# Packed first loads, another order of the first projection, and hand-placed side products in a two-layer decoder step

## The chip, the cores and the metric

The kernel runs on one core of one Trainium2 chip. A core has five engines that run beside each other and wait for one another through semaphores: TensorE (PE in the profile; PEld are its weight loads), VectorE (DVE), ScalarE (ACT), GpSimd (POOL) and SyncE (SP), which issues most of the transfers. Sixteen DMA engines carry the transfers of all queues. The metric is the device time of one execution in microseconds (us). Before the change it is 618.79 us, the median of three runs (618.44 to 619.36).

## What is computed

One inference step of a decoder with two layers, for 256 prompt rows and 8 sample rows (one new token each, with 256 past tokens in pages of 128) that share all weights. In fp32; model width 1024, 8 heads of 64 per attention, feed-forward width 2816.

```python
# layer 0                                         # for prompt rows and sample rows
h = rmsnorm(x, norm_g);  z = h @ w_in             # w_in: 1024 x 2560
q, k, v, bu, bv = split(z)                        # 512 columns each
q, k = rope(q), rope(k)
a = softmax(q k^T / 8, causal, incl. past) v      # 256-blocks; with these sizes all past is seen
bvn = layer_norm(gelu(bv), sgu_gain)
b = gelu(bu) * (tril(sgu_w) @ bvn + sgu_b)        # mixes rows in chunks of 128
x = x + concat(a, b) @ w_out                      # 1024 x 1024
x = x + (gelu(causal_conv3(h2 @ w_gate)) * (h2 @ w_up)) @ w_down,  h2 = rmsnorm(x)
# layer 1: the same frame with w_in of 1024 x 2048 (q, k, v, u), stick-breaking attention
# and a pooling mixer; at the end a final rmsnorm
```

Outputs are the normed rows, the new k and v, the new bvn rows of the samples, and the pooling and convolution states.

## The kernel before

**Layout.** Everything is held transposed: a tile of 128 features by 264 columns (256 prompt rows and 8 sample rows). A weight is cut into blocks of 128 x 128; the host packs the 1472 blocks in the order in which they are used (`_phases`, line 95, and `_pack_weights`, line 123). The kernel walks that list once (`run`, line 310): block after block, three matmuls each, because both operands are split into a high part (rounded to fp32r) and a low part (the rest): high weight by high data (L329), high by low (L330), low by high (L331). So the first projection (in0) has 160 blocks and 480 matmuls, the first output projection (out0) 64 blocks and 192 matmuls. "Block 32" below is the 33rd block of that list.

**Weights.** Eight blocks are a weight tile. `raw` (line 275) loads 8 or 16 blocks by one transfer from SP's queue into a pool of three buffers (`rawp`), `split` (line 290) makes the high part `wh` on ScalarE (L306) and the low part `wl` on VectorE (L307), up to three tiles ahead, in four buffers. The first tile is split by VectorE in three pieces (L303, L304), and its load is cut in three as well. A fourth load of raw weights has to wait until the first buffer is free again.

**The first data.** The input and the norm's gain come in four transfers from ScalarE's queue (line 345). Each of the eight input tiles is multiplied by the gain and split (`operand_tile`, line 371: L373 on ScalarE, L374 on VectorE). The squares of the tiles (L386) are added up on GpSimd (L395, L398); a matmul with ones (L406) and Ln and Exp on ScalarE (L408, L409) give the factor R = 1/rms, which is applied to the results of the projection, not to its input. Eight matmuls on a constant (`warm`, L357) run before the data are there.

**The first projection.** Its order is q, k, bv, bu, v, four output tiles each (`in0`, line 97). For the first four output tiles the list goes over the five first input tiles in the outer loop (`q0`, `KQ = 5`), so that it can start with little data; then each output tile takes its eight blocks in one go. A result is in one of four PSUM banks of the pool `psm` (tag `mm`) until `in0_evac` (line 630) has taken it: for q and k a shuffle (L635), a multiplication (L637 or L639), a multiplication on GpSimd (L640) and an addition (L641), for the others one multiplication with R (L643). All need R.

**Side products.** The four other PSUM banks (`psa`, tag `at`) serve the small matmuls: scores of the prompt (`s_qk`, line 655), softmax (`s_soft`), transposes (`s_tr`), products with v (`s_av`), the same for the samples (`sm_score`, `sm_soft`, `sm_tr`, `sm_out`), and the gating mixer (`gm_mean`, `gm_var`, `gm_norm`, `gm_tr`, `gm_gate`). Each is hung on the list by a number (`hk.at`, lines 796 to 836): `hk.at(n, f)` means that f is written down after 8(n+1) blocks. What follows from that is decided by a scheduler that simulates a timeline when the kernel is built; it may put a product later, and it interleaves its matmuls with those of the list. Only what `tc.keep_in_program_order` marks stays where it is written. On the chip each engine then goes through its own list strictly in order.

**Queues.** SP's queue issues the weights, the constants, and the pages of the caches: 16 page numbers are read from the page table into registers (`value_load`, line 424) and 32 pages of 256 KB are loaded for layer 0 (K, then V). A transfer that waits for a buffer holds up what stands behind it on that queue.

Of the kernel before, what the change touches and what calls it, by code (L numbers as in the profile page):

```python
# [9 lines left out]
F32 = mybir.dt.float32  # L10
# [8 lines left out]
P = 128  # L19
# [19 lines left out]
PINM = 8  # L39
SQL = 2  # L40
XD = (1, 2, 4, 8)
WARM = 8
YD = ((0, 1), (1, 3), (3, 5), (5, 7), (7, 8))

SC0 = 9
SGL = 6
GG = 16
GM = 12
GV = 13.5
GN = 16.1  # L50
SQK = 5
STR = 7
SSO = 9.5
STP = 12
GT = 17
GA = 17.5
VP = 17
SAV = 18
AVS = 18.5
MSK = 4.5  # L60
KL = 0
VL = 9
SQ = 4
SMO = -0.5
# [30 lines left out]
def _phases():  # L95
    k8 = list(range(KD))
    in0 = [(n, t) for n in ("q", "k", "bv", "bu", "v") for t in range(4)]
# [25 lines left out]
def _pack_weights(w_in0, w_out0, w_in1, w_out1, gate, up, down):  # L123
# [28 lines left out]
    return np.concatenate(out)  # L152
# [18 lines left out]
def _consts():  # L171
# [19 lines left out]
    h8 = np.arange(8)  # L191
# [8 lines left out]
    add("sm", (used & (h32[:, None] // 2 == h8[None, :])).astype(f))  # L200
    add("hs", (used & ((2 * g32 + h32 % 2)[:, None] == (np.arange(512) // 64)[None, :])).astype(f))
# [7 lines left out]
    ("w", (_NB * P * P,)), ("x", (P, KD + KD * T)), ("vec", (P, _NVEC)), ("cst", _CST_ARR.shape), ("rope", (P, 2 * T)),  # L209
# [12 lines left out]
def tile_decoder_step(ctx: ExitStack, tc: tile.TileContext, a):  # L222
    nc = tc.nc
    v, s, g, pe = nc.vector, nc.scalar, nc.gpsimd, nc.tensor
# [22 lines left out]
    XG = con.tile([P, KD + KD * T], F32, name="XG")  # L247
    GAIN = XG[:, :KD]
    X = XG[:, KD:].rearrange("p (m t) -> p m t", t=T)
# [5 lines left out]
    PALL = con.tile([P, 4, NS, 16], F32, name="PALL")  # L255

# [17 lines left out]

    def raw(ci):
        if ci not in raws:
            n = _CHUNKS[ci] * P
            r = rawp.tile([P, n], F32, tag="raw", name=f"raw{ci}")
            o = coff[ci] * P * P
            src = a["w"][o:o + P * n].rearrange("(p f) -> p f", p=P)  # L280
            raws[ci] = r
            if ci == 0:
                return lambda c, e: nc.sync.dma_start(r[:, c * P:e * P], src[:, c * P:e * P])
            nc.sync.dma_start(r, src)
        return raws[ci]
# [4 lines left out]
    def split(t):  # L290
        for tt in range(len(splits), min(t + (LOOK if pos[0] else 0), NT - 1) + 1):
# [5 lines left out]
            h = wsp.tile([P, 8 * P], F32R, tag="wh", name=f"wh{tt}")  # L297
            l = wsp.tile([P, 8 * P], F32R, tag="wl", name=f"wl{tt}")
            splits[tt] = (h, l)
            if tt == 0:  # L300
                def piece(c, e, h=h, l=l, src=src):
                    c, e = c * P, e * P
                    tc.keep_in_program_order(v.tensor_copy(h[:, c:e], src[:, c:e]))  # L303
                    tc.keep_in_program_order(v.tensor_tensor(l[:, c:e], src[:, c:e], h[:, c:e].bitcast(F32), ALU.subtract))  # L304
                return piece
            s.activation(h, src, AF.Copy)  # L306
            v.tensor_tensor(l, src, h.bitcast(F32), ALU.subtract)  # L307
        return splits[t]

    def run(order, rhs, evac, hooks=None):  # L310
# [5 lines left out]
        for m, k in order:  # L316
# [4 lines left out]
            if m not in ps:  # L321
                ps[m] = psm.tile([P, 512], F32, tag="mm", name=f"mm{i}")
                first = True
            else:
                first = False
# [9 lines left out]
            while hooks and n >= 8 * (hooks[0][0] + 1):  # L335
                for f in hooks.pop(0)[1]:
                    f()

    orders = dict(_PHASES)


    CS = f4("ropecs", (P, 2, T))
    xcut = [0] + [KD + e * T for e in XD]
    for b, e in zip(xcut, xcut[1:]):
        nc.scalar.dma_start(XG[:, b:e], a["x"][:, b:e])
    part = raw(0)
    part(0, 2)
    part(2, 4)
    part(4, 8)
    raw(1)  # L350
    raw(2)
    s.preload_act_table_set("natural_log_exp_and_others")
    warm = con.tile([P, 512], BF16, name="warm")
    v.memset(warm, 1.0)
    pw = at("warm")
    for i in range(WARM):
        tc.keep_in_program_order(pe.matmul(pw, warm[:, :P], warm, start=i == 0, stop=i == WARM - 1))  # L357

    def late(dst, src):
# [729 lines left out]
```

## Time and profile before

| what | value |
|---|---|
| median of 3 runs | 618.79 us |
| the profiled execution | 618.47 us |
| its span, first to last instruction | 616.4 us |
| mean granted TensorE clock | 0.996 |
| weight transfers of 1024 KB | 89, of 512 KB 5 |
| DMA moved | 121.40 MB, mean 197 GB/s |
| start of block 0, 32, 160 and 192 (first matmul of each) | 4.51, 24.92, 90.57, 110.39 us |

The span is the stretch from the first to the last instruction; the 2.1 us by which the execution is longer lie around it. In the views each row of a group gives the line of the kernel, the engine, the operation, what is written and read, its shape and count, then busy time and mean duration. A matmul is pipelined: the duration in its row (some 280 ns) is longer than the distance from one matmul to the next (some 120 ns), so what a matmul costs is read from start to start. On VectorE and ScalarE, too, the next instruction starts before the one in front of it ends, by some 0.08 to 0.1 us. An idle time in brackets names what ended it.

### The profile page before, as it was taken

How to read it: one execution, taken by the hardware profiler on the slowest of the kernel's cores; microseconds unless marked ns; L12 is line 12 of the kernel's file. 1: busy time of each engine (PE TensorE's matmuls, PEld its weight loads, DVE VectorE, ACT ScalarE, POOL GpSimd, SP SyncE). 2: the span in 40 equal slices, each digit the busy share in tenths (PEclk: the TensorE clock that was granted, in tenths of full speed). 3: DMA queues.
4: the chain of work that ended last, by engine and by line, in shares of the span. 5: the costliest groups of instructions: out<-in, count | busy, mean ns of one | idle time of the engine just before them, and what ended most of it. 6: DMA issues, size and time to landing. Idle time of an engine off the chain costs nothing.

```text
span 616.4 us, 12351 instructions
## 1 busy us (share of the span) xinstructions
PE 599.4 (97%) x4924; PEld 575.3 (93%) x4924; DVE 413.1 (67%) x704; ACT 350.4 (57%) x621; POOL 84.9 (14%) x111
## 2 busy tenths in 40 slices
PE   7899999999999999999999999999999999999994
PEld 5788987999999999999999997899999999999994
DVE  6986663969976676655555686396996766764441
ACT  5459763767756555644442757376765555554441
POOL 3330132324200000001110000042420000001020
PEclk9999999999999999999999999999999999999998
DMA  7995873543655445695477559944364555554502
GB/s 259 325 403 220 328 258 54 206 153 133 216 184 205 158 184 205 228 392 200 155 229 262 219 184 141 134 175 172 136 215 170 200 182 167 199 189 166 200 1 70
DMA packets 41354, 121.40 MB, mean 197 GB/s; under 512 B 17490, under 2 KB 19410, under 8 KB 29906
## 3 DMA queue, kind: packets, MB, share of 16 engines
q1 hardware_dynamic: 40178, 119.00, 59.3%
q10 hardware_dynamic: 1120, 1.63, 0.9%
q8 instruction: 38, 0.62, 0.4%
q14 instruction: 18, 0.15, 0.1%
HBM read 116.67 MB, written 3.94 MB: 196 GB/s over the span
## 4 chain that ended last, share of the span: by engine, by line
PE 84%; DVE 7%; issue 3%; DMA 2%; ACT 2%; POOL 1%; SPq 0%; DVEq 0%; ACTq 0%
PE mm L330 26%; PE mm L329 25%; PE mm L331 25%; DMA raw<-in_w 2%; DVE wl L307 2%; DVE xn_l L374 1%; PE pv_l L465 1%; PE sc L451 1%; PE pav L494 1%; PE Z L900 1%; DVE wk L542 1%; ACT wh L306 1%; PE Z L884 1%; POOL wk L553 0%; PE pt L684 0%
## 5 line engine op out<-in xcount | busy, mean ns | idle before, releaser
L307 DVE TENSOR_TENSOR wl<-raw,wh 128x1024 fp32r<-128x1024 f32 x183 | 229.4, 1255 | 129.1 <-ACT wh L306 129.0
L306 ACT ACTIVATE wh<-raw 128x1024 fp32r<-128x1024 f32 x183 | 193.7, 1059 | 182.5 <-PE mm L330 169.3
L330 PE MATMUL mm<-xn_l,wh 128*128 128x264 f32 x544 | 154.7, 284 | 1.7 <-DVE xn_l L374 1.5
L329 PE MATMUL mm<-xn_h,wh 128*128 128x264 f32 x544 | 153.8, 283 | 0.0
L331 PE MATMUL mm<-xn_h,wl 128*128 128x264 f32 x544 | 153.4, 283 | 0.0
L330 PEld LDWEIGHTS mm<-xn_l,wh 128*128 128x128 f32 x544 | 102.3, 188 | 2.5 <-DVE xn_l L374 2.5
L329 PEld LDWEIGHTS mm<-xn_h,wh 128*128 128x128 f32 x544 | 102.1, 188 | 0.0
L331 PEld LDWEIGHTS mm<-xn_h,wl 128*128 128x128 f32 x544 | 102.1, 188 | 0.0
L330 PE MATMUL mm<-a_l,wh 128*128 128x264 f32 x352 | 99.8, 284 | 0.0
L329 PE MATMUL mm<-a_h,wh 128*128 128x264 f32 x352 | 99.5, 284 | 0.0
L331 PE MATMUL mm<-a_h,wl 128*128 128x264 f32 x352 | 99.4, 283 | 0.0
L331 PEld LDWEIGHTS mm<-a_h,wl 128*128 128x128 f32 x352 | 66.2, 188 | 0.0
L330 PEld LDWEIGHTS mm<-a_l,wh 128*128 128x128 f32 x352 | 66.2, 188 | 0.0
L329 PEld LDWEIGHTS mm<-a_h,wh 128*128 128x128 f32 x352 | 66.0, 188 | 0.0
L329 PE MATMUL mm<-xg_h,wh 128*128 128x264 f32 x160 | 46.6, 298 | 3.6 <-DVE q L637 1.6
L330 PE MATMUL mm<-xg_l,wh 128*128 128x264 f32 x160 | 46.1, 293 | 0.0
L331 PE MATMUL mm<-xg_h,wl 128*128 128x264 f32 x160 | 44.7, 291 | 1.3 <-DVE wl L307 1.3
L329 PE MATMUL mm<-xg_f_h,wh 128*128 128x264 f32 x160 | 45.8, 286 | 0.0
L330 PE MATMUL mm<-xg_f_l,wh 128*128 128x264 f32 x160 | 45.4, 284 | 0.0
L331 PE MATMUL mm<-xg_f_h,wl 128*128 128x264 f32 x160 | 45.3, 283 | 0.0
L329 PE MATMUL mm<-xg_n_h,wh 128*128 128x264 f32 x128 | 37.4, 292 | 0.0
L331 PE MATMUL mm<-xg_n_h,wl 128*128 128x264 f32 x128 | 36.8, 288 | 0.0
(266 smaller groups left out, 1074.5 us busy)
## 6 DMA issues: line engine op xcount, KB each, us to landing
raw<-in_w SPq DMA_DIRECT2D x89, 1024.0 KB, 4.8
K<-in_kt SPq DMA_DIRECT2D x32, 256.0 KB, 6.0
V<-in_vp SPq DMA_DIRECT2D x32, 256.0 KB, 5.6
raw<-in_w SPq DMA_DIRECT2D x5, 512.0 KB, 5.3
CST<-in_cst SPq DMA_DIRECT2D x1, 548.0 KB, 5.5
XG<-in_x ACTq DMA_DIRECT2D x1, 528.0 KB, 7.8
out_k<-k SPq DMA_DIRECT2D x1, 528.0 KB, 9.4
out_v<-v SPq DMA_DIRECT2D x1, 528.0 KB, 3.0
```

The lines of the kernel that those rows point to most:

```text
L306: s.activation(h, src, AF.Copy)
L307: v.tensor_tensor(l, src, h.bitcast(F32), ALU.subtract)
L329: pe.matmul(o, h[:, c:c + P], xh, start=first, stop=False)
L330: pe.matmul(o, h[:, c:c + P], xl, start=False, stop=False)
L331: pe.matmul(o, l[:, c:c + P], xh, start=False, stop=left[m] == 0)
L374: j = v.scalar_tensor_tensor(l, src, gain, h.bitcast(F32), ALU.mult, ALU.subtract)
L451: pe.matmul(ps[32 * t:32 * t + 32, :PAST].rearrange("p (g k) -> p g k", g=NPG), qz[:, t, sq, :], kt[sq][:, :, t * P:(t + 1) * P], start=sq ...
L465: pe.matmul(pv[32 * j:32 * j + 32, :], pz[:, pg, sq, :], vtiles[sq][:, pg, :], start=pg == 0, stop=pg == NPG - 1)
L494: pe.matmul(o, vt[:, 0, h * HD:(h + 1) * HD], w[:, :SEQ], start=True, stop=False)
L542: v.scalar_tensor_tensor(C[:, 1:SEQ], G[:, 0:SEQ - 1], wc(1, j), C[:, 1:SEQ], ALU.mult, ALU.add)
L884: tc.keep_in_program_order(pe.matmul(ps[:, 0:SEQ], kh[:, 0:P], qh[:, 0:SEQ], start=False, stop=False, skip_group_check=True))
L900: pe.matmul(ps[:, 0:384], negU, x, start=False, stop=False, skip_group_check=True)
```

## The change

The change is confined to what happens up to the end of out0, with three small exceptions named at the end.

1. **Packed first loads.** The gain, the eight input tiles and the first 16 weight blocks are packed into one array `xw` on the host (`_FIRST`, `_pack_first`) and come by six transfers, each with the weight blocks and the input tile that go together: two blocks and tile 0 with the gain, two blocks and tile 1, then three times four blocks and one tile, then tiles 5 to 7. Transfers 1 and 3 go from ScalarE's queue, the others from SP's. The weights of blocks 16 to 47 no longer go through the pool of three buffers, but into tiles of the general pool `up`. The page table comes on ScalarE's queue at the start, and the 16 page numbers are read on SP's queue between the first weight loads. The weight loads keep their written place on SP's queue. The residual needs the input once more, so it is loaded again into `X` in four transfers of 264 KB at blocks 120 to 144 (`late_x`).
2. **Order of the first projection.** bv, q, k, bu, v. ScalarE makes the high parts of the first weights but for the first two blocks; all of this is in a written order (`part`, `whole`). The norm is finished after block 30 (`norm0`); the results of the first four output tiles are held in their banks until then. The first two q tiles (blocks 32 and 40) use banks of the other pool (`spare`).
3. **Side products at chosen blocks.** `blk(b, f)` puts f after b blocks, and while `fixed` is set, which is during in0 and out0, all matmuls and transposes keep their written order. The numbers stand in the diff. The products of the probabilities with v, all four, now come after block 8 of out0.
4. **Work moved between engines.** The second multiplication of rope, the sums of squares of the gating mixer and its last multiplication go from GpSimd to VectorE; one of the two scalings of the probabilities from ScalarE to VectorE; the masks and the sample's q from VectorE to ScalarE. The table of ScalarE for gelu is loaded twice, once for bv early and once for bu, and the other table loaded behind each.
5. **Smaller matmuls.** The mask is added to the first and the last 128 of the 384 columns of a score tile, where it was added to all (in layer 1 as well); the four small matmuls of `sm_tr` on `hs` become one. Warm-up is 12 matmuls of 256 columns where it was 8 of 512.

Outside in0 and out0 are the narrower masks of layer 1 and the fixed place of one copy (`negU`); the scheduler also places some ten instructions of layer 1's attention by one or a few places differently.

```diff
-    in0 = [(n, t) for n in ("q", "k", "bv", "bu", "v") for t in range(4)]
+    in0 = [(n, t) for n in ("bv", "q", "k", "bu", "v") for t in range(4)]
...
+_FIRST = [((0, 2), (0, 1)), ((2, 4), (1, 2)), ((4, 8), (2, 3)), ((8, 12), (3, 4)), ((12, 16), (4, 5)), ((0, 0), (5, 8))]
...
+    class TensorE:
+        @staticmethod
+        def keep(i):
+            return tc.keep_in_program_order(i) if fixed[0] else i
...
-            r = rawp.tile([P, n], F32, tag="raw", name=f"raw{ci}")
+            r = f4(f"raw{ci}", (P, n)) if ci < C8 else rawp.tile([P, n], F32, tag="raw", name=f"raw{ci}")
...
-        for tt in range(len(splits), min(t + (LOOK if pos[0] else 0), NT - 1) + 1):
+        for tt in range(len(splits), min(t + (2 if t == 3 else LOOK), NT - 1) + 1):
...
+    spare = (32, 40)
-                ps[m] = psm.tile([P, 512], F32, tag="mm", name=f"mm{i}")
+                ps[m] = at(f"mm{i}") if i in spare else psm.tile([P, 512], F32, tag="mm", name=f"mm{i}")
...
-    for b, e in zip(xcut, xcut[1:]):
-        nc.scalar.dma_start(XG[:, b:e], a["x"][:, b:e])
+    for i in range(len(_FIRST)):
+        r = f4(f"xw{i}", (P, n))
+        tc.keep_in_program_order((s if i in (1, 3) else nc.sync).dma_start(r, a["xw"][o:o + P * n].rearrange("(p f) -> p f", p=P)))
+        if i == 4:
+            raw(2)
+    tc.keep_in_program_order(s.dma_start(PT, a["pt"]))
+    for c in (3, 4):
+        raw(c)
+        page_regs(2)
+    late(CS, a["rope"].rearrange("p (c t) -> p c t", c=2))
+    raw(5)
+    page_regs(4)
+    late(CST, a["cst"])
+    raw(6)
+    page_regs(4)
+    late(VEC, a["vec"])
+    page_regs(4)
...
+    low = part(0, v)
+    operand_tile(xg[0], 0, xin[0], GAIN[:, 0:1], pin=True)
+    low()
+    for m in range(1, 5):
+        part(m, s)()
+        operand_tile(xg[m // 4], m, xin[m], GAIN[:, m:m + 1], pin=True)
+        if m != 2:
+            nrm.add((m - 1) // 2 if m < 4 else 2, xin[(m - 1) // 2 if m < 4 else 2])
+    whole(2)
+    for m in range(5, KD):
+        operand_tile(xg[m // 4], m, xin[m], GAIN[:, m:m + 1], pin=True)
+    for m in range(3, KD):
+        nrm.add(m, xin[m])
+        if m == 4:
+            whole(3)
+        elif m == 6:
+            whole(4)
...
+        if not R0:
+            held.append((m, o))
+            return
-            g.tensor_tensor(z, z, rope[:, 2 if n == "q" else 1, :], ALU.mult)
+            v.tensor_tensor(z, z, rope[:, 2 if n == "q" else 1, :], ALU.mult)
...
-            pe.matmul(ps[:, :384], identb, maskb0, start=True, stop=False, skip_group_check=True)
+            pe.matmul(two(ps), identb, two(maskb0), start=True, stop=False, skip_group_check=True)
...
-        g.tensor_tensor(bu4[:, t, :], bu4[:, t, :], bv4[:, t, :], ALU.mult)
+        v.tensor_tensor(bu4[:, t, :], bu4[:, t, :], bv4[:, t, :], ALU.mult)
...
+    fixed[0] = True
+    blk = lambda b, f, *x: hk.at(b / 8 - 1, f, *x)
+    for n in range(8):
+        blk(24 + 8 * n, drip_of(kload, 2))
+        blk(80 + 8 * n, drip_of(vload, 2))
+    for m in range(0, KD, 2):
+        blk(120 + 4 * m, late_x, m)
+    blk(30, norm0)
+    blk(40, masks)
+    blk(44, gm_first)
+    blk(72, sm_q)
+    for t, b in enumerate((82, 95, 108, 121)):
+        blk(b, s_qk, t)
+    for t, b in enumerate((103, 116, 129, 142)):
+        blk(b, s_tr, 2 * t)
+        blk(b, s_tr, 2 * t + 1)
+    blk(96, sgu_load)
+    blk(100, gm_mean)
+    blk(108, gm_var)
+    blk(131, sm_score)
+    blk(131, sm_soft)
+    blk(131, gm_gelu)
+    blk(130, gm_norm)
+    blk(140, sm_tr)
+    blk(144, lambda: nc.sync.dma_start(a["k0"], k4))
     for t in range(4):
+        blk(150, gm_tr, t)
+    blk(155, gm_own)
     for t in range(4):
+        blk(155, gm_gate, t)
+    for t, b in enumerate((146, 154, 162)):
+        if b <= 160:
+            blk(b, lambda t=t: v_pair(vt, v4[:, t, :], t, "v0"))
+    for i, b in enumerate((157, 159)):
+        blk(b, sample_av_of(st0, PZ, vtiles, i, "l0"))
     run(orders["in0"], pick(xg), in0_evac, hk)
...
+    blk(4, sm_out)
+    for t in range(4):
+        blk(8, s_av, t)
```

302 lines of the change are left out of this document (144 added, 158 removed).

## The prediction

> **What bounds the kernel now.** I read the page first (busy times, chain by engine), then the busy times by window, the waits of PE and of SP's queue, and the timeline of the first 25 us. The page, then two windows (columns: length; busy time and count of PE, PEld, DVE, ACT, POOL; clock; DMA share; GB/s):
>
> ```profile
> span 616.4 us, 12351 instructions
> PE 599.4 (97%) x4924; PEld 575.3 (93%) x4924; DVE 413.1 (67%) x704; ACT 350.4 (57%) x621; POOL 84.9 (14%) x111
> ```
> ```profile
> 110.00:250.00 140.00, 139.14 (x1147) 138.66 (x1146) 108.37 (x180) 86.70 (x157) 20.21 (x20) 1.00 0.50 178
> 500.00:600.00 100.00, 100.00 (x831) 100.00 (x830) 57.48 (x82) 52.02 (x81) 6.88 (x5) 1.00 0.46 160
> ```
>
> PE is the bound. At 831 matmuls in 100 us one costs 0.1203 us, a weight block of three 0.361. Behind out0 PE hardly pauses, DVE and ACT have reserve and DMA runs at half, so what PE is ahead at the end of out0 it keeps to the end. Time can be won up to there only; these are the places where it is lost (waits: us, times, longest; then the timeline: start, duration, in brackets the idle time and what ended it):
>
> ```profile
> PE mm L329 <- DVE q L637: 1.6, 1, 1.6
> PE mm L329 <- ACT wh L306: 1.3, 1, 1.3
> PE mm L331 <- DVE wl L307: 1.3, 1, 1.3
> PE mm L329 <- ACT catB_h L413: 0.7, 1, 0.7
> PE mm L329 <- DVE wh L303: 0.6, 1, 0.6
> PE S L658 <- ACT p L672: 0.3, 1, 0.3
> ```
> ```profile
> 4.51 0.98 PE L329 MATMUL mm<-xg_h,wh 128*128 128x264 f32 x2
> ...
> 6.33 0.42 PE L329 MATMUL mm<-xg_h,wh 128*128 128x264 f32 x1
> 6.55 0.42 PE L330 MATMUL mm<-xg_l,wh 128*128 128x264 f32 x1
> ...
> 24.92 0.36 PE L329 MATMUL mm<-xg_h,wh 128*128 128x264 f32 x1 [1.60 <-DVE q L637]
> ```
>
> Blocks 0 to 31 take 24.92 − 4.51 = 20.41 us where 96 matmuls at 0.1203 take 11.55. The excess is 8.9: four waits of 0.6, 1.3, 1.3 and 1.6 (4.8); the norm's matmuls (start 19.36, next matmul of the list 20.05: 0.7); a slow beginning, with a matmul each 0.22 (6.33 to 6.55) up to about 7, some ten of them 0.1 over the pitch (1.0); the rest in small gaps.
>
> **The supply in the first 25 us.**
>
> ```profile
> 0.00:5.00 5.00, 3.54 (x9) 1.47 (x10) 1.89 (x8) 2.23 (x3) 1.16 (x8) 1.00 0.55 162
> 5.00:10.00 5.00, 4.29 (x25) 3.80 (x23) 3.59 (x8) 1.63 (x5) 0.79 (x1) 1.00 1.00 357
> 10.00:15.00 5.00, 3.70 (x26) 3.28 (x27) 3.87 (x5) 4.87 (x11) 2.65 (x3) 1.00 0.80 252
> 20.00:25.00 5.00, 3.40 (x27) 3.16 (x26) 4.62 (x18) 2.25 (x4) 0.84 (x2) 1.00 0.96 311
> 25.00:30.00 5.00, 5.00 (x42) 5.00 (x43) 4.41 (x11) 2.67 (x3) 1.47 (x4) 1.00 1.02 383
> ```
> ```profile
> SPq L284 <- DVE wl L307: 20.7, 5, 8.4
> ```
> ```profile
> 3.92 1.16 ACT L373 ACTIVATE xg_h<-XG 128x264 fp32r<-128x264 f32 x2
> 4.07 0.29 DVE L303 CAST wh<-raw 128x256 fp32r<-128x256 f32 x1 [2.12 <-DMA raw<-in_w]
> 10.13 1.06 ACT L306 ACTIVATE wh<-raw 128x1024 fp32r<-128x1024 f32 x1 [1.19 <-DMA raw<-in_w]
> ```
>
> SP's queue stood 20.7 us on the pool of three buffers. The DMA engines moved 0.81 MB by 5 us and 2.60 MB by 10. Input, gain and 16 blocks are 2.13 MB: moved by 5 + (2.13 − 0.81)/0.357 = 8.7, but released at 10.1. So a load is usable 1.4 after its bytes have moved.
>
> **Term 1, first loads and first stage.** Bytes ahead of block 16 stay the same; the first step needs two transfers of 264 KB together where 136 and 128 KB sufficed. I take 4.9 for the first matmul (now 4.51). Then 11.55, 1.0 for the slow beginning, 0.7 for the norm's matmuls and some waits. The 1.6 us on a PSUM bank moves back, since block 32 gets a spare bank; the waits on raw weights shrink, since blocks 16 to 47 need no buffer. I take 1.9 of the 4.8 (ends 0 and 4.8). Block 32: 4.9 + 11.55 + 1.0 + 0.7 + 1.9 = 20.05, 4.9 earlier (ends 6.8 and 2.0).
>
> **Term 2, what then becomes late.** The order in which the engines get their work shows it: the high part of raw load 6 (the first of 1024 KB) stands on ACT ahead of Ln and Exp of R, and its low part on DVE ahead of rope and of all results that need R. Then DVE has, before k tile 0 is ready: 3 operations for rope, 4 results of bv, five tiles of four operations (q0 to q3, k0), and about 6 low parts. The scores `s_qk` for head pair 0 stand at block 82, need k0, and PE's order is fixed there: PE waits, with all of its blocks behind it.
>
> ```profile
> L641 DVE TENSOR_TENSOR q<-q,rz_q 128x264 f32<-128x264 f32 x4 | 1.5, 423 | 0.0
> L307 DVE TENSOR_TENSOR wl<-raw,wh 128x1024 fp32r<-128x1024 f32 x183 | 229.4, 1255 | 129.1 <-ACT wh L306 129.0
> L307 DVE TENSOR_TENSOR wl<-raw,wh 128x1024 fp32r<-128x1024 f32 x10 | 13.8, 1384 | 4.9 <-ACT wh L306 4.9
> L640 POOL TENSOR_TENSOR rz_q<-rz_q,rope 128x264 f32<-128x264 f32 x4 | 3.0, 782 | 9.8 <-DVE rope L610 6.3 <-DVE rz_q L635 3.5
> ```
> ```profile
> 17.67 0.48 SPq L424
> ...
> 19.14 0.02 SPq L284
> ...
> 19.19 5.33 DMA raw<-in_w
> 24.61 1.07 ACT wh L306
> ```
>
> The second L307 row is of 24 to 60 us, where GpSimd works beside DVE. Neighbours overlap by 0.08 to 0.1, so a small operation costs 0.34 and a low part 1.17 (overall mean; GpSimd has nothing in that stretch after the change). After the landing: 1.1 for the high part, 1.2 for the low part, 27 × 0.34 = 9.2, 6 × 1.17 = 7.0; together 18.5.
>
> When does load 6 land? Through it 5.93 MB must come (2.13 packed, 2.10 raw 2 to 5, 0.27 rope, 0.38 constants, 1.05 itself). After 10 us that is 3.33 MB; at the 311 GB/s of 20 to 25 us it has moved by 20.7 and lands at 22.1; at 383, 20.1; at 252, 24.6. SP's queue allows it: eight page numbers precede the load, two take 19.14 − 17.67, so 5.9 in all, from about 9 (the page table taken to land behind the packed loads issued before it, 2.13 MB moved by 8.7) to 15.9 with four issues of 0.4–0.5; plus 5.33 as in the row it is 21.5.
>
> So k0 at 22.1 + 18.5 = 40.6. PE reaches block 82 at 20.05 + 50 × 0.361 = 38.1 and waits 2.5 (ends 0.5 and 5.0). The two terms are coupled: each us that block 32 comes later up to 22.5 is taken out of that wait. Terms 1 and 2 give −4.9 + 2.5 = −2.4, and load 6 sets it.
>
> **Term 3, waits at the side products.** The 0.7 (L413) and the 0.3 (L658) between blocks 32 and 224 go, since gating and products with v are placed anew: −1.0. But with PE's order fixed each side product that isn't ready stops PE, where the scheduler had put blocks ahead. No such wait is in this trace; ends 0 and 3 (four as long as the 0.7). I take 1.0. Together 0.
>
> **Term 4, smaller matmuls.**
>
> ```profile
> 43.76 0.18 PE S L658
> 43.94 0.42 PE S L660 x4
> ...
> 66.51 0.79 PE pO L724 x8
> ```
>
> A mask of 384 columns costs 0.18; with 256 of them 0.12. Eight in each layer: −0.96. Eight records of `pO` at 0.1 become two: −0.6. Together −1.5 (ends 0, were they in PE's shadow, and −1.6).
>
> **Edits at nothing, and their cover.**
>
> ```profile
> 60.00:70.00 10.00, 10.00 (x93) 9.47 (x86) 5.43 (x11) 7.72 (x16) 0.00 (x0) 1.00 0.84 314
> 80.00:90.00 10.00, 9.91 (x85) 9.42 (x84) 7.38 (x14) 5.12 (x10) 3.47 (x5) 1.00 0.71 248
> L790 POOL TENSOR_TENSOR bu<-bu,bv 128x264 f32<-128x264 f32 x1 | 1.7, 1656 | 1.7 <-ACT vt L490 1.7
> ```
>
> Squares, the gating multiplication and the scaling go to DVE, busy 5.4 to 7.4 of 10 where they fall; without that reserve each costs its 0.34. The multiplication of `bu` with `bv` leaves the 1.66 on GpSimd, which preceded the 0.7 wait. Masks and gelu's tables on ACT lie under its free 2 to 5 of 10. The second load of x (1.08 MB, 2.7 us at 400 GB/s) goes where DMA has a fifth free; if it held the weights, it would cost those 2.7. The warm-up ends before the data come.
>
> **Sum** against the profiled execution (618.47; 2.1 of it around the span): −2.4 + 0 − 1.5 = −3.9, 614.6. The median is 0.3 above it: 614.9, and I say **615.0**.
>
> **Two rules of the Trainium skill.** The rows at 3.92 and 4.07 show first pieces of two queues landing side by side, though 1060 KB stood on ACT's queue. "DMA: Bandwidth & Descriptors", section Queues, rings and completion order, says that each DMA engine takes turns between the queues that have work; this trace agrees. By it the page table comes sooner; what that gives is the fourth rival. The low part takes 1.38 beside GpSimd, 1.26 over the whole kernel. "SBUF — State Buffer", section SBUF: two separate sides, says that a VectorE operation with two SBUF inputs and one of GpSimd that reads SBUF shut each other out; the two rows agree. Were the longer time the low part's own in this stretch, six of them would add 0.8: 615.8.
>
> **Rivals.**
> 1. *Load 6 is late, and the kernel slower.* Place: Ln of R on ACT, behind that high part. Each us past 22.1 costs one us at block 82; beyond 26.0 nothing is left, beyond 27.2 it is slower by over 0.2%. For it: DMA already runs full at 5–10 us, and the page reads precede the load. Against: 383 GB/s is possible. At 5.6 late (a landing like 27.7, half again the 10 to 22.1 estimate) 620.6.
> 2. *The fixed order stalls* 3 us more than I take, at transposes or products whose DVE or ACT work is late: 618. For it: DVE is full from 24 to 40. Against: 5 of 10 free at 60.
> 3. *The early loads bring nothing*: block 32 stays at 24.9, since bytes rather than buffers set it. Then no wait at block 82: −1.0 + 1.0 − 1.5 = −1.5, 617.3.
> 4. *Queues share in turn*: the page table, third on ACT's queue behind two packed loads, lands by about 7.1 and not at 8.9 (an estimate: 1.8 us is 0.65 MB at 357 GB/s, about what is then still open of the packed loads on SP's queue); load 6 is issued and lands some 1.3 earlier, k0 too: 613.7.
>
> **Chances.** Forecast 0.57 (own range 613.2 to 617.5), rival 1 0.12, rival 2 0.10, rival 3 0.06, rival 4 0.15. Within 0.2% (1.24 us, about what a measurement can tell from no change) means 617.55 to 620.0. Faster: 0.55 + 0.15 + 0.04 = 0.74. Same: 0.02 + 0.02 + 0.07 + 0.02 = 0.13. Slower: 0.10 + 0.03 = 0.13. The range 612.8 to 619.6 reaches down past rival 4 (load 6 at 20.1) and up past rival 2.
>
> **What would show it.** Right: block 32 near 20; no wait on L637 or L413; one PE wait near block 82 for DVE's k, near 40.6; load 6 landing at 22, Ln of R at 23; masks at 0.12. Wrong: load 6 past 26; waits of over 1 us at transposes or products with v; a wait for raw weights at blocks 48 to 80 or 120 to 150; block 224 not near 118.

## The result and the profile after

| | before | after |
|---|---|---|
| median, four executions each | 618.62 us | 612.80 us (612.54 to 613.31) |
| the profiled execution, its span | 618.47, 616.4 us | 613.31, 610.6 us |
| start of block 0 | 4.51 | 4.89 |
| start of block 32 | 24.92 | 20.31 |
| start of block 82 | 47.75 | 40.02 |
| start of block 160 (out0) | 90.57 | 87.94 |
| start of block 224 (behind out0) | 122.04 | 115.59 |
| end of the list's last matmul | 607.36 | 601.72 |

The kernel is 5.8 us faster: ratio 0.9908, interval 0.9892 to 0.9923. (The median of before has moved from 618.79 to 618.62 by one more execution.) Block starts are those of the first of a block's three matmuls in the timeline.

The page of the changed kernel, and the waits of PE up to 125 us, warm-up left out (us, times, longest):

```profile
span 610.6 us, 12320 instructions
PE 598.7 (98%) x4922; PEld 577.3 (95%) x4922; DVE 416.7 (68%) x719; ACT 350.3 (57%) x623; POOL 71.4 (12%) x93
```
```profile
PE mm L228 <- ACT xg_h L399: 0.9, 1, 0.9
PE S L228 <- DVE k L703: 0.3, 1, 0.3
```

PE is the bound as before. All six waits that the prediction quoted are gone. Two are new: the first matmul (0.9), and the wait for k0 at block 82, 0.3 us. (All matmuls now have the line of the helper, L228.)

The timeline of the changed kernel at the places that decide:

```profile
4.89 0.59 PE L228 MATMUL mm<-xg_h,wh 128*128 128x264 f32 x1 [0.95 <-ACT xg_h L399]
...
10.10 0.42 PE L228 MATMUL mm<-xg_h,wh 128*128 128x264 f32 x1
10.32 0.39 PE L228 MATMUL mm<-xg_l,wh 128*128 128x264 f32 x1
10.54 0.29 PE L228 MATMUL mm<-xg_h,wl 128*128 128x264 f32 x1
10.66 0.28 PE L228 MATMUL mm<-xg_h,wh 128*128 128x264 f32 x1
...
20.31 0.28 PE L228 MATMUL mm<-xg_h,wh 128*128 128x264 f32 x1
20.46 1.06 ACT L312 ACTIVATE wh<-raw 128x1024 fp32r<-128x1024 f32 x1 [3.73 <-PE mm L228]
21.43 0.46 ACT L436 ACTIVATE R_n<-ns_n,epst 128x264 f32<-128x264 f32 x1
21.92 0.42 ACT L437 ACTIVATE R_n<-R_n 128x264 f32<-128x264 f32 x1
...
38.68 0.43 DVE L703 TENSOR_TENSOR k<-k,rz_k 128x264 f32<-128x264 f32 x1
39.16 0.93 PE L228 MATMUL S<-k,q 64*128 64x128 f32 x8 [0.28 <-DVE k L703]
```

Three things are to be seen. The first matmuls take 0.22 us each up to 10.5, longer than before (up to 7). From then on PE goes without a wait to the scores at block 82. And the chain that the prediction named stands there in one piece: high part of load 6 (20.46), Ln, Exp, and 16.4 us later the last addition of k0, for which PE waits. The row of the high part names PE as what ended ScalarE's idle time; the runs below show that it was the load.

How early the data came (columns as in the prediction; then a wait and an issue on SP's queue):

```profile
5.00:10.00 5.00, 5.00 (x21) 4.71 (x22) 4.71 (x10) 4.86 (x12) 1.35 (x2) 1.00 1.04 420
10.00:15.00 5.00, 5.00 (x41) 5.00 (x40) 5.00 (x6) 4.84 (x10) 3.15 (x5) 1.00 0.96 331
15.00:20.00 5.00, 5.00 (x40) 4.87 (x39) 3.73 (x3) 1.37 (x2) 1.52 (x1) 1.00 0.78 265
```
```profile
SPq L353 <- DMA PT<-in_pt: 1.9, 1, 1.9
```
```profile
12.96 0.44 SPq L287 DMA_DIRECT2D raw<-in_w  x1
```

420 GB/s moved between 5 and 10 us where it was 357, and load 6 was issued at 12.96.

### The profile page after: what moved, and what is told of

It is laid out like the page before. It is cut to its first block, busy times and chain, and to the rows that moved or that the text cites. A ratio compares the mean times of both kernels' runs of the same rounds, so it can differ in the third digit from the quotient of the medians.

```text
span 610.6 us, 12320 instructions
## 1 busy us (share of the span) xinstructions
PE 598.7 (98%) x4922; PEld 577.3 (95%) x4922; DVE 416.7 (68%) x719; ACT 350.3 (57%) x623; POOL 71.4 (12%) x93
## 4 chain that ended last, share of the span: by engine, by line
PE 70%; DVE 6%; issue 1%; ACT 1%; POOL 0%; DVEq 0%; ACTq 0%
PE mm L228 66%; PE Z L228 2%; DVE xn_l L400 2%; DVE wl L313 1%; PE pv_l L228 1%; PE sc L228 1%; DVE wk L576 1%; PE pav L228 1%; DVE wk L572 0%; DVE wk L577 0%; DVE X L1112 0%; DVE wk L586 0%; DVE a_l L448 0%; DVE wk L578 0%; PE pm L228 0%
## 5 line engine op out<-in xcount | busy, mean ns | idle before, releaser
L313 DVE TENSOR_TENSOR wl<-raw,wh 128x1024 fp32r<-128x1024 f32 x179 | 221.6, 1239 | 127.2 <-ACT wh L312 126.9
L312 ACT ACTIVATE wh<-raw 128x1024 fp32r<-128x1024 f32 x179 | 189.5, 1059 | 175.4 <-PE mm L228 169.6
L228 PE MATMUL mm<-xn_l,wh 128*128 128x264 f32 x544 | 155.2, 285 | 1.6 <-DVE xn_l L400 1.5
L228 PE MATMUL mm<-xn_h,wl 128*128 128x264 f32 x544 | 154.0, 284 | 0.0
L228 PE MATMUL mm<-xn_h,wh 128*128 128x264 f32 x544 | 153.8, 283 | 0.0
L228 PEld LDWEIGHTS mm<-xn_l,wh 128*128 128x128 f32 x544 | 102.2, 188 | 2.5 <-DVE xn_l L400 2.5
L228 PEld LDWEIGHTS mm<-xn_h,wh 128*128 128x128 f32 x544 | 102.3, 188 | 0.0
L228 PEld LDWEIGHTS mm<-xn_h,wl 128*128 128x128 f32 x544 | 102.0, 188 | 0.0
L228 PE MATMUL mm<-a_l,wh 128*128 128x264 f32 x352 | 99.7, 284 | 0.0
L228 PE MATMUL mm<-a_h,wl 128*128 128x264 f32 x352 | 99.5, 283 | 0.0
L228 PE MATMUL mm<-a_h,wh 128*128 128x264 f32 x352 | 99.5, 284 | 0.0
L228 PEld LDWEIGHTS mm<-a_h,wl 128*128 128x128 f32 x352 | 66.2, 188 | 0.0
L228 PEld LDWEIGHTS mm<-a_h,wh 128*128 128x128 f32 x352 | 66.1, 188 | 0.0
L228 PEld LDWEIGHTS mm<-a_l,wh 128*128 128x128 f32 x352 | 66.1, 188 | 0.0
L228 PE MATMUL mm<-xg_h,wh 128*128 128x264 f32 x160 | 48.5, 303 | 0.9 <-ACT xg_h L399 0.9
L228 PE MATMUL mm<-xg_l,wh 128*128 128x264 f32 x160 | 46.5, 291 | 0.0
L228 PE MATMUL mm<-xg_h,wl 128*128 128x264 f32 x160 | 46.5, 291 | 0.0
L228 PE MATMUL mm<-xg_f_h,wh 128*128 128x264 f32 x160 | 45.7, 286 | 0.0
L228 PE MATMUL mm<-xg_f_l,wh 128*128 128x264 f32 x160 | 45.4, 284 | 0.0
L228 PE MATMUL mm<-xg_f_h,wl 128*128 128x264 f32 x160 | 45.3, 283 | 0.0
L228 PE MATMUL mm<-xg_n_h,wh 128*128 128x264 f32 x128 | 37.4, 292 | 0.0
L228 PE MATMUL mm<-xg_n_h,wl 128*128 128x264 f32 x128 | 36.6, 286 | 0.0
```

What stands on the lines that cost most here:

```text
L228: return self.keep(nc.tensor.matmul(*x, **k))
```

## The experiments

Two theories on what sets the end of this stage. **A**, that of the prediction: load 6 sets R, R sets k0, and k0 sets block 82, so what is won earlier is lost in the wait there. **B**: the high part ahead of Ln waits for PE to free its buffer, as the row at 20.46 says, so whatever speeds PE up speeds up everything. Times are medians; the changed kernel's is 612.80, that of before lay at 618.37, 618.62 and 618.92 in the three sets of runs.

### Longer warm-up

```diff
-WARM = 12
+WARM = 16
```

> Warm-up of 16 matmuls instead of 12, so that PE has no pause before its first matmul with data (in the changed kernel warm-up ends at 3.94, the first matmul starts at 4.89, and a matmul takes 0.22 us up to 10.4). If the pause keeps the slow pace, the 0.22 ends near 7 and block 32 starts 1.0 to 1.5 us earlier than 20.31. Theory A (load 6 sets the factor R, and R with VectorE's work sets k0): k0 stays at 39.1, PE's wait for k at block 82 grows from 0.3 to 1.3-1.8, and the time stays within 0.3 us of 612.8. Theory B (the high part ahead of Ln waits for PE, as the row of the waits names it): R comes with PE, and the time falls by 1.0 to 1.5 us. If the pause isn't the cause, block 32 stays at 20.3.

Measured: 613.07 (612.66 to 613.91). PE's waits and the high part of load 6, in the timeline:

```profile
PE S L228 <- DVE k L703: 1.9, 1, 1.9
PE mm L228 <- DVE wl L640: 0.6, 1, 0.6
PE mm L228 <- ACT xg_h L399: 0.3, 1, 0.3
```
```profile
22.04 1.06 ACT L312 ACTIVATE wh<-raw 128x1024 fp32r<-128x1024 f32 x1 [4.80 <-DMA raw<-in_w]
```

The matmuls at 0.22 us are gone and block 16 starts 1.6 us earlier; block 32 only 0.4, since a low part (0.6) is now late. Nothing of it reaches the end. In this execution load 6 also came 1.6 later than in the profile above (here the row names the DMA), and the wait for k0 grew to 1.9. B fails: PE was ahead and R came later all the same.

### R ahead of load 6

On ScalarE, the high part of the first half of load 6 is put behind Exp.

```diff
-            s.activation(h, src, AF.Copy)
+            i = s.activation(h, src, AF.Copy)
+            if tt == 6:
+                behind(i, last[0])
```

> Ln and Exp of R ahead of the high part of load 6 on ScalarE. Theory A: R no longer waits for load 6 and is ready near 21.2 instead of 22.3; k0 is up to 1.1 us earlier and the wait of 0.3 goes: 612.3 to 612.6. Rival: the low part that VectorE does later only changes places with the results, k0 comes at the same time and the time stays at 612.8, or PE waits at block 48 for the high part.

Measured: 617.13 (613.46 to 619.54, twelve executions; the profiled one, 613.46, is the fastest), 4.3 slower than the changed kernel and above what either theory expected. VectorE's timeline:

```profile
20.21 0.43 DVE L667 TENSOR_TENSOR rope<-ropecs,R_n 128x264 f32<-128x264 f32 x1 [1.34 <-ACT R_n L439]
...
37.78 0.45 DVE L699 STREAM_SHUFFLE rz_k<-mm 128x264 f32<-128x264 f32 x1
38.13 0.41 DVE L703 TENSOR_TENSOR k<-mm,rope 128x264 f32<-128x264 f32 x1
38.47 1.21 DVE L315 TENSOR_TENSOR wl<-raw,wh 128x1024 fp32r<-128x1024 f32 x1
39.60 0.42 DVE L705 TENSOR_TENSOR k<-k,rz_k 128x264 f32<-128x264 f32 x1
```

R was there 2.2 us earlier (rope starts at 20.21, in the changed kernel 22.70 behind a low part), and yet k0's last addition came 0.9 later: the scheduler, given another order on ScalarE, made another one for VectorE, in which a shuffle, a multiplication and a low part of later tiles stand ahead of it. PE waited 1.7 us there. So the edit did not test what it was meant to: an earlier R was used up by another order on VectorE. What it shows is that VectorE's list between R and k0 counts as R does. Why its executions spread over 6 us is taken up below.

### Both

The two diffs above together.

> Both edits. Theory A: alone neither gives more than 0.5 us, together 0.9 to 1.5 (611.3 to 611.9), since the faster start is used up waiting for k0 unless k0 comes earlier too. Theory B: no more than the longer warm-up alone gives.

Measured: 617.06 (614.42 to 619.54, twelve executions). In its profile (614.42, the fastest) the wait for k0 is 1.7 again, and one of 0.8 at the gating's mean is new. The 0.9 to 1.5 expected did not come, for the reason just given.

### Load 6 later

```diff
     late(CST, a["cst"])
+    late(X, a["x"].rearrange("p (m t) -> p m t", t=T))
     raw(6)
```

> One more transfer of 1.08 MB (the input once more, unused) ahead of load 6 on SP's queue; everything else stands in the same order. At 380 GB/s load 6 lands 2.8 us later, near 23.2. Theory A: Ln, R, k0 and the wait at block 82 move by 2.8 (wait near 3.1): 615.6. Theory B and the claim that loads are not the limit: up to no change (612.8 to 613.5).

Measured: 615.40 (614.67 to 617.12). The timeline, two windows around the first slow matmuls, and two waits of PE, of the profiled execution (617.12, the slowest of five):

```profile
23.53 1.06 ACT L312 ACTIVATE wh<-raw 128x1024 fp32r<-128x1024 f32 x1 [6.50 <-DMA raw<-in_w]
...
42.12 0.93 PE L228 MATMUL S<-k,q 64*128 64x128 f32 x8 [1.88 <-DVE k L704]
42.98 0.59 PE L228 MATMUL mm<-xg_h,wh 128*128 128x264 f32 x1
43.36 0.42 PE L228 MATMUL mm<-xg_l,wh 128*128 128x264 f32 x1
43.58 0.42 PE L228 MATMUL mm<-xg_h,wl 128*128 128x264 f32 x1
```
```profile
42.00:46.40 4.40, 4.28 (x23) 3.95 (x24) 3.80 (x12) 1.54 (x8) 0.00 (x0) 0.61 0.95 353
46.40:50.00 3.60, 3.60 (x34) 3.35 (x34) 2.99 (x9) 2.15 (x5) 0.00 (x0) 1.00 1.06 401
```
```profile
PE S L228 <- DVE k L704: 1.9, 1, 1.9
PE mm L228 <- ACT identb L684: 1.6, 1, 1.6
```

The median is 2.6 above the changed kernel, where A said 2.8 and B nothing; only SP's list had changed. Load 6 set block 82: it came 3.1 later, and block 82 3.0. A had the wait at block 82 at 3.1; 1.6 of the loss was taken earlier, at block 48 (27.37). Its row names ScalarE's copy of the identity, but VectorE's results of bv, which free the banks and need R, begin at 26.80, 0.57 ahead of it; in the next run they begin 0.58 ahead (28.46 and 29.04), and there the row names them. One thing more: after the pause of 1.88 us fourteen matmuls took 0.22 us each, with the granted clock at 0.61 in that window, 1.4 us that no wait shows.

### The buffers of blocks 16 to 47

```diff
-            r = f4(f"raw{ci}", (P, n)) if ci < C8 else rawp.tile([P, n], F32, tag="raw", name=f"raw{ci}")
+            r = rawp.tile([P, n], F32, tag="raw", name=f"raw{ci}")
```

> Weights of blocks 16 to 47 back in the pool of three buffers, the rest as changed. Load 6 then waits for the low part of tile 3 (ends 15.3 in the changed kernel), is issued near 15.4 instead of 12.96 and lands near 22.9; ScalarE's order also has the masks ahead of Exp (1.0). Theory A: R and k0 come 2.5 to 3.5 us later, PE's pause at block 82 grows to 2.8-3.8, and such a pause can bring the slow pace back as in the run with a late load 6 (15 matmuls, 1.5 us): 615.3 to 618. If the buffers bring nothing by themselves: 612.8 to 613.3.

Measured: 621.60 (619.56 to 622.70), slower than the kernel before. Waits of PE and the timeline of ScalarE:

```profile
PE mm L228 <- DVE bv L705: 2.7, 1, 2.7
PE S L228 <- DVE k L703: 2.1, 1, 2.1
```
```profile
23.53 1.06 ACT L312 ACTIVATE wh<-raw 128x1024 fp32r<-128x1024 f32 x1 [1.65 <-DMA raw<-in_w]
24.50 0.46 ACT L436 ACTIVATE R_n<-ns_n,epst 128x264 f32<-128x264 f32 x1
...
26.80 0.41 ACT L437 ACTIVATE R_n<-R_n 128x264 f32<-128x264 f32 x1
```

Direction and chain as in A, but 3.6 more than its upper end. R came 4.9 late (Exp at 26.80): 3.1 by load 6 and the rest by the masks and a high part in between. At that delay the four banks of bv, which R has to free, stop PE at block 48 (2.7) before k0 does (2.1). In the profile (619.56, the fastest) nine matmuls at 0.22 us follow the second pause, and later PE waits 0.6 at the gating's mean.

### Old small matmuls

```diff
-            pe.matmul(two(ps), identb, two(maskb0), start=True, stop=False, skip_group_check=True)
+            pe.matmul(ps[:, :384], identb, maskb0, start=True, stop=False, skip_group_check=True)
...
-        pe.matmul(pO[:, :4 * NS], cst("hs"), st0["ow"], start=True, stop=True)
+        for t in range(4):
+            pe.matmul(pO[:, t * NS:(t + 1) * NS], cst("hs"), st0["ow"][:, t * NS:(t + 1) * NS], start=True, stop=True)
```

(The masks of layer 1 likewise, and the middle of both masks is set to zero.)

> Masks again on all 384 columns in both layers, and the samples' small product again as four matmuls. By the prices of the prediction (0.06 each for 16 masks, 0.6) 1.4 us slower, less 0.1 for the first two, which PE may do while it waits for k0: 614.0 to 614.3. Rival: these matmuls lie in waits of PE, no more than 0.4: 612.8 to 613.2.

Measured: 614.66 (613.90 to 615.96), 1.9 slower. In its profile load 6's high part starts 0.5 later by itself (20.99) and block 82 0.4 later; from there to block 224 another 1.0 is lost and 0.6 behind it: 1.6 for the matmuls, against 1.4 expected. They lie on PE's path.

### The scheduler's placing

```diff
-    fixed[0] = True
+    fixed[0] = False
```

> PE's side products are placed by the scheduler again, at the same block numbers at the earliest. Theory A: the gain lies in the first loads and not in the fixed order; PE has more changes between the list and side products (some 25 at 0.05 to 0.1), but need not stop at block 82: 612.8 to 614.5. Rival: the fixed order itself brings 2 us or more: 614.8 and above.

Measured: 613.55 (612.55 to 614.89), 0.75 above the changed kernel, less than either kernel's spread. Block 82 comes 1.8 earlier, since the scheduler puts the scores later; that is gone by block 160, which starts 1.7 later, and out0 begins and ends with that. PE has no wait from 82 to 125 us in either. At block 224 this kernel is 1.9 behind, and 0.8 of that comes back behind out0, without a wait. So the fixed order is worth 1.9 us up to there and little at the end.

### The same pieces in separate transfers

```diff
-        tc.keep_in_program_order((s if i in (1, 3) else nc.sync).dma_start(r, a["xw"][o:o + P * n].rearrange("(p f) -> p f", p=P)))
+        src = a["xw"][o:o + P * n].rearrange("(p f) -> p f", p=P)
+        if w_:
+            tc.keep_in_program_order(nc.sync.dma_start(r[:, g_:g_ + w_], src[:, g_:g_ + w_]))
+        if g_:
+            tc.keep_in_program_order(s.dma_start(r[:, :g_], src[:, :g_]))
+        tc.keep_in_program_order(s.dma_start(r[:, g_ + w_:], src[:, g_ + w_:]))
```

> The same first pieces in separate transfers, weights on SP's queue, input and gain on ScalarE's. Bytes and buffers stay. ScalarE issues seven transfers at 0.45 ahead of its table load (1.28), so its first operation starts near 5.2 instead of 4.32 and PE starts 0.9 later; load 6 is hardly touched. Theory A: block 32 0.5 to 1.5 later, k0 within 0.5, so the time within 0.7 of 612.8. Rival: packing as such is the gain: 614.8 or more.

Measured: 617.72 (616.90 to 619.09), 4.9 slower. ScalarE's timeline and the waits of SP's queue up to 20 us:

```profile
6.86 0.48 ACTq L372 DMA_DIRECT2D PT<-in_pt  x1
7.38 1.28 ACT L386 ACT_TABLE_LOAD   x1 [7.38 <-DMA xw<-in_xw]
8.68 0.51 ACT L404 ACTIVATE xg_h<-xw 128x264 fp32r<-128x264 f32 x1
...
26.19 1.06 ACT L312 ACTIVATE wh<-raw 128x1024 fp32r<-128x1024 f32 x1 [4.91 <-DMA raw<-in_w]
```
```profile
SPq L353 <- DMA PT<-in_pt: 5.5, 1, 5.5
```

The expectation failed twice over. The last three issues on ScalarE's queue came at 4.25, 5.58 and 6.86, 1.3 us apart, where the first four were 0.4 to 0.5 apart; the one at 4.25 directly follows the landing of an earlier piece of that queue (4.23), and the others look like the same wait. So ScalarE's first operation on data came at 8.68 and not 5.2, and the page table, the last of them, was issued at 6.86 instead of 1.67. SP then stood 5.5 us before the first page number, and load 6 was issued 5 us late. Block 32 starts 3.9 later, but block 82 5.6 later: what counts is the load again. This run does not separate packing from the place of the page table.

### The old order of the projection

```diff
-    in0 = [(n, t) for n in ("bv", "q", "k", "bu", "v") for t in range(4)]
+    in0 = [(n, t) for n in ("q", "k", "bv", "bu", "v") for t in range(4)]
...
-    blk(44, gm_first)
+    blk(100, gm_first)
...
-    blk(100, gm_mean)
-    blk(108, gm_var)
+    blk(106, gm_mean)
+    blk(112, gm_var)
```

> First projection again in the order q, k, bv, bu, v, with the packed loads; the gating's first steps moved from blocks 44, 100 and 108 to 100, 106 and 112. VectorE has four results of bv (1.4 us) less ahead of k0, but frees the four banks of q later (two operations each, behind low parts), and the gating chain starts later. Theory A: k0 about 1.4 earlier, no pause at block 82, waits of up to 1 us for a bank at block 48 to 64 and for the gating ahead of out0: 612.5 to 615. Rival: the order is what makes the early start possible: 615 or more.

Measured: 621.44 (620.77 to 623.07). The wait of PE that carries it:

```profile
PE pmu L228 <- DVE bsum L814: 6.9, 1, 6.9
```

Up to block 96 the kernel is level with the changed one (46.56 against 46.51). The loss comes at the gating's mean, which I had put too early: VectorE ends its sum at 62.5, PE stood there since 55.6, with all of its list behind it. So its time says nothing for or against the order; it shows what a fixed place ahead of its data costs: 6.9 us, and eleven matmuls at 0.22 after it. Two things can be read off the profile all the same. Block 32 starts at 20.34 (20.31 in the changed kernel), so the early start does not come from the order, which the rival had claimed. And k0's last addition starts at 37.16 where it was 38.68, although load 6's high part came 0.9 later (21.33), and PE does not wait for it.

### Rope's second multiplication on GpSimd

```diff
-            v.tensor_tensor(z, z, rope[:, 2 if n == "q" else 1, :], ALU.mult)
+            g.tensor_tensor(z, z, rope[:, 2 if n == "q" else 1, :], ALU.mult)
```

> The second multiplication of rope back on GpSimd. VectorE has five operations (1.7 us) less ahead of k0, but its low parts beside GpSimd may take 1.38 instead of 1.22 and each tile waits for GpSimd's 0.78. Theory A: k0 within 1 us of 39.1 either way, the time within 1 us of 612.8. Rival: GpSimd in the chain makes k0 2 us later: 614.8 or more.

Measured: 615.15 (613.89 to 619.05, ten executions; the profiled one 614.10). VectorE's timeline:

```profile
31.67 1.21 DVE L313 TENSOR_TENSOR wl<-raw,wh 128x1024 fp32r<-128x1024 f32 x1
...
35.54 1.76 DVE L313 TENSOR_TENSOR wl<-raw,wh 128x1024 fp32r<-128x1024 f32 x1
...
38.26 1.74 DVE L313 TENSOR_TENSOR wl<-raw,wh 128x1024 fp32r<-128x1024 f32 x1
39.91 0.42 DVE L703 TENSOR_TENSOR k<-k,rz_k 128x264 f32<-128x264 f32 x1
```

VectorE does five operations less (1.7 us) and k0 is still later: its last addition follows the high part of load 6 (21.20 in this execution) by 18.7 where it was 18.2. Low parts that meet a multiplication on GpSimd take up to 1.76 instead of 1.21. So the edit itself makes k0 0.5 later in this profile, and 0.7 more is load 6's own lateness. The median is 2.35 above the changed kernel, outside the 1 us of A; the 2 us at k0 of the rival are not in the profile either, and the rest lies in the spread of the executions.

### Load 6 earlier

```diff
     for c in (3, 4):
         raw(c)
-        page_regs(2)
     late(CS, a["rope"].rearrange("p (c t) -> p c t", c=2))
     raw(5)
-    page_regs(4)
-    late(CST, a["cst"])
     raw(6)
-    page_regs(4)
+    late(CST, a["cst"])
+    page_regs(12)
     late(VEC, a["vec"])
```

> Load 6 issued straight behind loads 3 to 5; the constants and all page numbers come after it; the lists of the other engines are the same. Theory A: load 6 lands 2 to 3 us earlier (near 18), its high part is done before the norm's sum (near 20), R comes at 21.2, so k0 at 38.0, and block 82 is set by PE's own work again: 39.5 where PE needs 39.5, no pause there. The time is 0.3 to 1.3 us below that of the changed kernel (611.5 to 612.5), and it spreads less, since landings of load 6 from 20.4 to 22 no longer matter. Rival: the page numbers, now read later, hold loads 7 and 8, and PE waits for raw weights: no gain or a loss.

Measured: 611.71 (611.70 to 612.36), ratio to the kernel before 0.9886 (0.987 to 0.9903). ScalarE's timeline, and all of PE's waits from the first matmul to 125 us:

```profile
16.88 1.06 ACT L312 ACTIVATE wh<-raw 128x1024 fp32r<-128x1024 f32 x1 [0.42 <-DMA raw<-in_w]
19.46 0.48 ACT L434 ACTIVATE R_n<-ns_n,epst 128x264 f32<-128x264 f32 x1 [1.52 <-PE ns_n L228]
```
```profile
PE mm L228 <- ACT xg_h L397: 1.1, 1, 1.1
```

A move of page numbers and constants on SP's queue, with every other list as it was, takes the wait for k0 away: Ln follows the norm's sum and no longer the load, k0's last addition starts at 37.24, and block 82 at 39.35. That is 1.1 us below the changed kernel, as A said, and none of its four executions is as slow as the fastest of that one's. (That it spreads less, 0.66 against 0.77, four executions can't tell.) It also rules out theory B by itself: the high part of load 6 starts at 16.88, 3.1 ahead of block 32 (19.99), so no matmul near that block holds it, as the row at 20.46 would have it, 0.15 behind the start of block 32, in the changed kernel. It is the fastest kernel with one edit.

### Load 6 earlier, and the longer warm-up

The diff above, and `WARM = 16`.

> The same with 16 warm-up matmuls. Theory A: with load 6 out of the way the faster start reaches the end where it was used up before: 1.0 to 1.8 us below the changed kernel (611.0 to 611.8). Rival: another limit takes over (VectorE's work from R to k0, 16.4 us long, full): no more than the early load alone.

Measured: 611.65 (611.39 to 612.56). The time lies in the range that A gave, but it is no more than the early load alone gives (611.71), so the faster start did not reach the end and A failed as an account. The wait that takes the gain:

```profile
PE mm L228 <- DVE wl L638: 0.6, 1, 0.6
```

Block 16 starts 1.0 earlier than with the early load alone (11.96 against 12.97), block 32 level (19.95 and 19.99): VectorE's low part for block 24 is late. Not R's chain but VectorE's splitting is what holds the first stage then.

### What the runs say together

Load 6 came at five different times, by chance or by an edit. Starts of its high part and of block 82, from the timelines, in the kernels whose lists on ScalarE and VectorE between the two are the same:

| kernel | high part of load 6 | block 82 | between |
|---|---|---|---|
| changed | 20.46 | 40.02 | 19.56 |
| old small matmuls | 20.99 | 40.43 | 19.44 |
| longer warm-up | 22.04 | 41.49 | 19.45 |
| load 6 later | 23.53 | 42.98 | 19.45 |
| separate transfers | 26.19 | 45.64 | 19.45 |

Over 5.7 us the distance stays within 0.12, while block 32 starts anywhere from 19.8 to 24.3. That is the chain of theory A, read from one profile of each kernel. The early load breaks it: there block 82 (39.35) lies 22.5 behind.

## Why the prediction was right, point by point

The prediction said 615.0, with a range of 612.8 to 619.6; the median is 612.8, at its lower end. The gain was 5.8 us and not 3.8.

1. **First stage: 20.05 forecast, 20.31 measured.** That they agree is luck: two errors cancel. The slow beginning was put at 1.0; 24 matmuls from 4.89 to 10.66 took 5.8 where 24 × 0.1203 is 2.9, so it cost 2.9. The waits put at 1.9 were all gone. The sum also left out, without a reason, the rest of the excess of before (8.9 less 4.8, 0.7 and 1.0 is 2.4); after the change 0.3 of such a rest is left (15.4 less 11.55, 2.9 and 0.7).
2. **Load 6: the mechanism held, the size was off, and this is the term that was mis-sized.** The work from the landing to k0 was put at 18.5; from the start of the high part (20.46) to k0 (38.68 + 0.43) it is 18.65. But load 6 was to land at 22.1, and its high part started at 20.46, within the ends given. PE was to wait 2.5 us at block 82 and waited 0.3: 2.2 of the error. Of these 1.5 are k0's (39.1 and not 40.6); the other 0.8 are PE's own, which came to the scores at 38.9 and not 38.1 (block 32 is 0.3 late, the two masks ahead of the scores take 0.4). What failed is the number of bytes moved by 10 us: 2.60 MB, taken over from before, where 215 and 420 GB/s in the two windows of 5 us make 3.18 MB. The 311 GB/s for the time after that was about right (298 from 10 to 20 us); with 3.18 MB the same working gives 20.2. The issue, put at about 15.9, came at 12.96, and from there to the high part it took 7.5 and not 5.33. (The prediction's own terms for the issue, 9 and 5.9 and four issues of 0.4 to 0.5, make 16.5 to 16.9; 15.9 and 5.33 make 21.2 and not 21.5; and half of the 12.1 from 10 to 22.1, in rival 1, is 6.1 and not 5.6. None of them enters the sum.)
3. **The fourth rival is what made the issue earlier.** SP waited 1.9 us for the page table, then read two numbers, and issued load 4 at 7.98; two reads took 1.47 before, so the table was there by about 6.5, where rival 4 had 7.1 and the sum 8.9. The rule of the Trainium skill that it rested on ("DMA: Bandwidth & Descriptors", section Queues, rings and completion order) agrees with that. The rival's 613.7 would have been the nearer number, and its load 1.3 us earlier is near the 1.6 measured; how much of the 1.6 comes from the early issue and how much from the bytes moved by 10 us was not separated.
4. **Waits at side products: 1.0 forecast, none measured.** The waits on L413 and L658 went, as said. Nothing came in their place: from behind the wait for k0 to 125 us PE waits for nothing. The 1.0 was chosen between 0 and 3 without a row that spoke for it.
5. **Smaller matmuls: 1.5 forecast, 1.6 measured** by undoing them.
6. **The sum with the measured terms** is −4.6 + 0.3 − 1.0 − 1.6 = −6.9 (block 32, the wait for k0, the two waits that went, the smaller matmuls). At block 224 the measured lead is 122.04 − 115.59 = 6.45, and 0.5 of layer 1's masks is still to come: 6.95. The prediction had named block 224 not near 118 as a sign of being wrong, and it starts at 115.59. The end shows 607.36 − 601.72 = 5.64. So some 1.3 us are given back over 485 us behind out0, where no wait is new. The loss isn't spread evenly: from block 352 to 544 each 64 blocks take 23.33 us where they took 23.20, from 1056 to 1312 23.33 where they took 23.15, 1.1 in all and less than 1 ns for each matmul. The prediction had taken a lead at block 224 as one that stays, and put this term at nothing. Why it doesn't stay wasn't tried. It is luck for the number: with the whole 6.9 the time would have been near 611.9, below the range.
7. **Rivals 1 to 3.** Load 6 is indeed the lever of rival 1: with load 6 3.1 us later the gain shrinks by 2.6, and with the old buffers, 4.9 late at R, the kernel is slower than before. In the changed kernel it came early enough. Rival 2 did not occur in the changed kernel, but a fixed place chosen badly cost 6.9 us. Rival 3 fell: block 32 starts 4.6 earlier.

What the change consists of, by undoing one part at a time, against 612.80: the buffers of blocks 16 to 47 are worth 8.8 us, the packing with the page table's place 4.9, rope on VectorE 2.35 (of which its profile shows 0.5), the small matmuls 1.9 (of which 0.4 may be load 6's chance lateness), the fixed order 0.75. The numbers don't add up to the 5.8, since several of them act through the same wait. Not undone by itself were the spare banks, the other work moved between engines and the place of the products with v; the order of the projection was, but the time of that run does not price it.

## What to carry to other kernels

Where a statistic has to come before any result can be used, follow back what stands ahead of it in each engine's list: here a weight's high part that nobody needed for another 5 us held the factor of the norm, and eight reads of page numbers, with a wait for the page table, and a load of constants held that weight. An earlier start of the bounding engine is worth only as much as the next thing it waits for is early too, so price both and take the later. When a transfer's landing decides, look for what the issuing queue does ahead of it; here moving it cost the other engines nothing.

## What the runs showed of the hardware that wasn't expected

- **PE's pace after a pause.** After a pause of 1.88 us (load 6 later), of 2.1 (old buffers) and of 6.9 (old order), matmuls took 0.22 instead of 0.12 us for some 2 to 3 us; after pauses of 1.92 (longer warm-up), 1.86 (rope on GpSimd), 1.9 (separate transfers) and even 2.7 (old buffers, at block 48) in the profiled executions they did not. So the length of the pause alone doesn't decide. At the start the slow pace ended at 8.4 to 10.5 us in the profiles of the changed kernel and of seven others with 12 warm-up matmuls and the same first transfers, and it was absent in one more (the scheduler's placing), so it differs between executions that begin alike; with 16 warm-up matmuls it was absent in two profiles and lasted to 9.9 in a third, where the pause ahead of the first matmul with data was 0.3 us as in one of the two. The Trainium skill ("TensorE: Matmul & The Clock Gate", Part 1) says that the clock's window runs freely and isn't reset by a kernel's start; such differences agree with that, and no run here shows the window itself. The granted clock in the window rows read 1.00 at the start even so, and 0.61 (load 6 later) and 0.66 (old buffers) only after the later pauses.
- **Spread.** Three kernels with a pause of 1.7 to 1.9 us at block 82 in their profile (R first, both edits, rope on GpSimd; ten or twelve executions each) spread over 5 to 6 us between executions, the one without any pause there over 0.7 (four executions). That a pause of this length sometimes brings the slow pace would explain it, and the clocks on record fit: in these three kernels the executions above 617 us have a mean granted clock of 0.990 to 0.995, those below 615 one of 0.995 to 0.998. Against it stands the longer warm-up, with a pause of 1.9 in its profile and a spread of 1.3 over four executions. The profiles show one execution each, so this is argued and not shown.
- **VectorE beside GpSimd.** A low part of 128x1024 took 1.21 alone and up to 1.76 when a multiplication on GpSimd ran, more than the 1.38 that the mean of before suggested. (Row 1.21 at 31.67, row 1.76 at 35.54.) Giving GpSimd work to relieve VectorE made VectorE later.
- **ScalarE's queue.** With eight transfers issued from it the last three came 1.3 us apart, the first of them right behind the landing of an earlier one (4.25 and 4.23), and the engine's own first operation on data stood behind them: 8.68, in the changed kernel 4.32.
- **A pace that depends on the program.** From block 224 to the list's last matmul the changed kernel takes 485.84 us (before 485.03, with wider masks), and nine further kernels made from it the same to within 0.1; with the scheduler's placing it is 485.04 and with the old order 485.39, and there, too, the difference lies in blocks 352 to 544 and 1056 to 1312, or in the second of these alone. No wait differs; it stays open.
